# Adaptive vectors by row sums on the Vector engine, from transposed weights

## The chip, the core and the metric

One core of a Trainium2 chip runs the whole program: one launch of some 21,000 instructions, all unrolled, on PE (matrix products), DVE (vector), ACT (scalar functions and copies) and POOL, with SP issuing most of the transfers. The metric is device time in microseconds. The kernel before takes 1334.85 us, the median of 3 runs (1333.11 to 1336.33).

## The reference

Two layers work on 512 latent tokens of width 1024, with 256 context tokens as a prefix. Layer 0 mixes by neighbourhood attention and a two-way gated recurrence (HGRN2), layer 1 by a short gated convolution; each ends in a convolutional gated feed-forward part. What matters here is the conditioning of each layer:

```
silu_c = jax.nn.silu(c)                              # (1, 1024)
mod = silu_c @ ada_w[layer] + ada_b[layer]           # ada_w[layer]: 1024 x 6144
shift_m, scale_m, gate_m, shift_f, scale_f, gate_f = jnp.split(mod, 6, axis=-1)
h = modulate(rms_norm(x, norm_mix_w[layer]), shift_m, scale_m)
x = x + gate_m[:, None, :] * y
h = modulate(rms_norm(x, norm_ffn_w[layer]), shift_f, scale_f)
x = x + gate_f[:, None, :] * conv_ffn(h, ...)
```

So each layer has six adaptive vectors of 1024 values, which are one product of a row with a 1024 x 6144 matrix.

## The kernel before

Activations lie transposed: 8 tiles of 128 channels by 512 tokens. A value per channel is then a value per partition, and `mod[:, l, c]` holds the 128 values of column block `c` (0 to 47) of layer `l`: shift_m is c 0 to 7, scale_m 8 to 15, gate_m 16 to 23, shift_f 24 to 31, scale_f 32 to 39, gate_f 40 to 47.

Each product of full precision runs as three PE matmuls (`mm3`, lines 287 to 290), on weights and activations that are split into a high and a low part. `Weights` loads the raw weights on SP's queue into two buffers (`wraw`); ACT casts the high part (line 92 or 125) and DVE subtracts it to get the low part (line 93 or 126), into three buffers of each. `get` and `ahead` set how far the splitting runs ahead of PE. A raw buffer can be loaded again when its last split on DVE is done.

In order of time: a prefix (norm, shift_m and scale_m of layer 0 on PE by `ada_tile`, the first projections `pq`), the projections and scans of the recurrence, the attention, the output projection, ffn_up of layer 0, ffn_down of layer 0 (`project_back` with `kgroups`, 640 to 760 us), od_in (the three projections of the short convolution, 760 to 950 us), od_out, ffn_up of layer 1, ffn_down of layer 1. Every engine works its instructions in order, and that order is set by a list scheduler that goes by program order and readiness; `pin` keeps an instruction behind all that were written before it on its engine.

The other adaptive vectors (the last four of layer 0, all six of layer 1) are worked out piece by piece beside all this, by the class `Ada` (lines 474 to 527). A job is 512 outputs, 20 jobs in all. One unit (`unit`) takes 128 of the 1024 inputs: SP loads 128 x 512 weights (`ar`, three buffers, loaded two units ahead), and DVE multiplies them by the 128 values of silu(c), one per partition (`sil[:, r, 0:1]`), and adds them to `aa` (line 504; line 502 for the first of a job). After 8 units DVE reduces `aa` across 32 partitions with a transposing reduction (line 508, `ad`), three calls later PE sums the four groups of partitions by a small product with `sel` (line 514, `gather`, `pad`), and two calls later DVE adds the bias in four pieces (line 520, `finish`). The reduction, the gather and the sums are not pinned.

Units are called from fixed places. `Weave` calls a unit after so many ticks of the projections (`ada_units`, lines 563 and 948); from the output projection on, `units(n)` stands between other work: in `project_back` (line 1053) behind the two weight tiles of a step and ahead of its products, in od_in behind each pair of tiles (lines 1283, 1291, 1300), and in ffn_up of layer 1 (line 1252).

At the end of ffn_up of layer 1 (lines 1319 to 1325) gate_f is laid out along the rows of all partitions: DVE multiplies the identity by 128 values, PE multiplies a matrix of ones by that diagonal, ACT copies the result out of PSUM.

Of the kernel before, what the change touches and what calls it, by code (L numbers as in the profile page):

```python
# [9 lines left out]
F32 = mybir.dt.float32  # L10
F32R = mybir.dt.float32r
BF16 = mybir.dt.bfloat16
I32 = mybir.dt.int32
# [161 lines left out]
def backbone(ctx: ExitStack, tc: tile.TileContext, a, out, dump=None):  # L175
# [65 lines left out]
    ws = Weights(nc, wp, plan)  # L241


    cst = cp.tile([P, 769], F32, name="cst")
    ident, sel = cst[:, 0:128], cst[:, 128:256]
    smask = cst[:, 256:769]
    hgm = cp.tile([P, 256], I32, name="hgm")
    ones = cp.tile([P, P], F32, name="ones")
    epsc = cp.tile([P, 1], F32, name="epsc")
    V.memset(ones[:], 1.0)  # L250
# [2 lines left out]
    vec = cp.tile([P, 372], F32, name="vec")  # L253
    pv, abT, fcv = vec[:, 0:100], vec[:, 100:196], (vec[:, 196:284], vec[:, 284:372])
    mod = cp.tile([P, 3, 48], F32, name="mod")
    sil = cp.tile([P, 8, 32], F32, name="sil")
    oml = cp.tile([P, 8], F32, name="oml")
    noml = cp.tile([P, 8], F32, name="noml")
    amul = cp.tile([P, 5, KT], F32, name="amul")
# [2 lines left out]

    m1 = ExitStack()
    mp = m1.enter_context(tc.tile_pool(name="mp", bufs=1))
    y0 = [yp.tile([P, 2, T], F32R, tag=f"y{k}", name=f"h0_{k}") for k in range(KT)]
    h0 = [(t[:, 0], t[:, 1]) for t in y0]
    hc4 = [mp.tile([P, 4, TC], F32R, tag="hc", name=f"hc{i}", bufs=4) for i in range(4)]
# [61 lines left out]
    with ExitStack() as st:  # L329
# [94 lines left out]
        for k in range(KT):  # L424
            fetch(k + 2)
            if k == 3:
                for i in range(2):
                    nc.sync.dma_start(ct[i][:].rearrange("p (k t) -> p k t", t=TC),
                                      ctxt[i * T : (i + 1) * T, :].rearrange("(k p) t -> p k t", p=P))
                nc.sync.dma_start(hgm[:], a["hgm"])  # L430
                nc.sync.dma_start(cst[:, 256:769], a["cst"][:, 256:769])
            conv(k + 1)
            modulated(h0[k][0], h0[k][1], xs[k][:], 0, k)
            if k + 1 < KT:
                ada_tile(k + 1, k + 2)
            wh, wl = w0[k]
            for m in range(6):
                ms = slice(m * P, (m + 1) * P)
                mm3(pq[m][:], wh[:, ms], wl[:, ms], h0[k][0], h0[k][1], k == 0, k == KT - 1)
                if k > 6 or (k == 6 and m % 2):  # L440
                    next(ctx_task, None)
                if k == KT - 1 and m in (2, 4):
                    ws.conv()
# [14 lines left out]
        for m in range(4):  # L458
            sg = sp.tile([P, T], F32, tag="sgq", name=f"sgq{m}", bufs=2)
            S.activation(sg[:], pq[m][:], AF.Sigmoid)  # L460
            V.tensor_tensor(qf[m], pq[m][:], sg[:], ALU.mult)
        for m in range(2):
            gate(m, pq[4 + m][:])
        for _ in ctx_task:
# [9 lines left out]
    class Ada:  # L474


        jobs = [(0, p_, j) for p_ in range(2, 6) for j in range(2)] + [(1, p_, j) for p_ in range(6) for j in range(2)]
        n, calls, raw, late = 0, 0, {}, []

        def load(self):  # L480
            n = len(self.raw)
            r = n % 8
            l, p_, j = self.jobs[n // 8]
            raw = ap_.tile([P, T], F32, tag="araw", name=f"ar{n}", bufs=3)
            nc.sync.dma_start(raw[:], ada_w[l][r * P : (r + 1) * P, p_ * D + j * T : p_ * D + (j + 1) * T])
            self.raw[n] = raw

        def unit(self, aux):
            self.calls += 1
            while self.late and self.late[0][0] <= self.calls:  # L490
                self.late.pop(0)[1]()
            if self.n >= 8 * len(self.jobs):
                return
            r = self.n % 8
            l, p_, j = self.jobs[self.n // 8]
            while len(self.raw) < min(self.n + 3, 8 * len(self.jobs)):
                self.load()
            raw = self.raw[self.n]
            self.n += 1
            if r == 0:  # L500
                self.acc = ap_.tile([P, T], F32, tag="aacc", name=f"aa{self.n}", bufs=1)
                pin(V.tensor_scalar(self.acc[:], raw[:], sil[:, 0, 0:1], None, ALU.mult))
                return
            pin(V.scalar_tensor_tensor(self.acc[:], raw[:], sil[:, r, 0:1], self.acc[:], ALU.mult, ALU.add))  # L504
            if r < 7:
                return
            red = ap_.tile([P, 16], F32, tag="ared", name=f"ad{self.n}", bufs=1)
            V.tensor_reduce(red[:], self.acc[:].rearrange("p (b j) -> p b j", j=32), axis=AX.X, op=ALU.add,
                            apply_transpose=True)
            pm = []  # L510

            def gather():
                pm.append(aux(f"pad{l}{p_}{j}"))
                TE.matmul(pm[0][:, 0:16], sel, red[:], start=True, stop=True)

            def finish():
                c = p_ * 8 + 4 * j
                for qd in range(4):
                    s4 = slice(32 * qd, 32 * qd + 32)
                    V.tensor_tensor(mod[s4, l, c : c + 4], pm[0][s4, qd:16:4], abT[s4, l * 48 + c : l * 48 + c + 4],  # L520
                                    ALU.add)
                if p_ in (1, 4):
                    w0 = (16 if p_ == 1 else 32) + 8 * l + 4 * j
                    V.scalar_tensor_tensor(amul[:, 2 * l + (1 if p_ == 1 else 2), 4 * j : 4 * j + 4], mod[:, l, c : c + 4],
                                           1.0, pv[:, w0 : w0 + 4], ALU.add, ALU.mult)

            self.late += [(self.calls + 3, gather), (self.calls + 5, finish)]

    ada = Ada()

# [25 lines left out]

    def ada_units(n, gap):
        for _ in range(n):
            ada.unit(aux_t)
            yield gap  # L560


    wv.add(ada_units(11, 6))
    for j in range(2):
        pl = [acc_t(f"pvl{j}{i}") for i in range(2)]
        pcx = aux_t(f"pvc{j}")
# [378 lines left out]

    wv.add(attention())
    wv.add(gated(), 20)
    wv.add(ada_units(43, 3))
    for p_ in range(1, 4):
        query(p_)  # L950
        key_value(p_)
# [83 lines left out]
    def project_back(nm, src, groups, gate, norm, start=0):  # L1035
# [5 lines left out]
        for n, (mp_, gi) in enumerate(steps):  # L1041
            k0, k1 = groups[gi]
            if gi == 0:
                o = [acc_t(f"pb{nm}{mp_}{i}") for i in range(2)]
            w = [ws.get(), ws.get()]
            first, lastg = gi == 0, gi == len(groups) - 1
            if n == len(steps) - 1:
                break
            if n == len(steps) - 2:
                ws.spare = [(gq, f"q{2 * i}", f"q{2 * i + 1}") for i in range(3)]  # L1050
                ws.ahead(4)
            if n < len(steps) - 2 or len(groups) > 1:
                units(4 if len(groups) == 1 else 5)
            for i in range(2):
                mms(o[i], w[i], src, k0, k0, k1, slice(0, T), first, lastg)
                if lastg:
                    norm.back(o[i], 2 * mp_ + i, slice(0, T), gate)
                    if mp_ or i:
                        norm.add(slice(0, T))
# [162 lines left out]

    def units(n):
        for _ in range(n):
            ada.unit(aux_t)

    def ffn_up(l, src, rest):
        g = []
        mv = []

        def gated_tile(f, oa, ov):
            col = lambda n: fcv[l][:, n : n + 1]
            tt = fp.tile([P, T], F32, tag="t", name=f"cv{l}{f}", bufs=5)
            conv3(tt, oa, col(f), col(22 + f), col(44 + f), col(66 + f))
            S.activation(tt[:], tt[:], AF.Gelu)
            gh, gl = gtiles(l, f)
            V.tensor_tensor(ov[:], ov[:], tt[:], ALU.mult)
            split(gh, gl, ov[:])
            g.append((gh, gl))

        def before():
            rest()
            mv.extend(differences(l, src))

        oa, ov = quad(f"a{l}", src, before, lambda: mv[1]())
        for i in range(2):
            gated_tile(i, oa[i], ov[i])
        for j in range(1, FT // 2):
            for i, (ra, rv) in enumerate(group(f"{l}{j}", mv[0])):
                gated_tile(2 * j + i, ra, rv)  # L1250
            if l and j < 9:
                units(2)
        return g

    mix = [mixn[p_] for p_ in range(4)] + [mixg[h] for h in range(4)]
# [22 lines left out]
    for j in range(4):  # L1278
        if j == 0:
            oc, ou = quad("c", nrm.h, rest)  # L1280
        else:
            oc = pair(f"c{j}", nrm.h)
            units(3)
        cs = []
        for i in range(2):
            t = gp.tile([P, T], F32, tag=f"g{16 + i}", name=f"cs{j}{i}")
# [1 line left out]
            cs.append(t)  # L1288
        if j:
            ou = pair(f"u{j}", nrm.h)  # L1290
            units(3)
        ts_ = []
        for i in range(2):
            m = 2 * j + i
# [2 lines left out]
            conv3(t, cs[i], rowv(76 + m, 1), rowv(84 + m, 1), rowv(92 + m, 1), rowv(68 + m, 1))  # L1297
            ts_.append(t)
        ob = pair(f"b{j}", nrm.h)
        units(3)  # L1300
        for i in range(2):
            m = 2 * j + i
            mh = gp.tile([P, T], F32R, tag=f"g{2 * m}", name=f"mch{m}")
# [79 lines left out]
def layout(inputs):  # L1383
# [5 lines left out]
    for l in range(2):  # L1389
# [3 lines left out]
    arrays["upq"] = np.ascontiguousarray(np.stack([  # L1393
        np.concatenate([blk(0, 2, 1), blk(2, 4, 1), blk(0, 2, 0), blk(2, 4, 0)], -1),
        np.concatenate([blk(4, 8, 0), blk(4, 8, 1)], -1)], 2))
    arrays["vec"] = np.ascontiguousarray(np.concatenate([np.asarray(v).reshape(-1, P) for v in vecs], 0).T)
    rpb = np.asarray(inputs["na_rpb"])[0].reshape(4, 2, 15, 31)
    rp = np.zeros((4, 15, 2, WPAD), rpb.dtype)
# [29 lines left out]
```

## Time and profile before

| what | value |
|---|---|
| runs, median of 3 | 1334.85 us (1333.11 to 1336.33) |
| the profiled execution | 1333.99 us, of which the span from first to last instruction is 1332.2 us |
| PE busy | 98% of the span |
| weight loads of PE | 86% |
| DVE busy | 72% |
| ACT busy | 47% |
| mean DMA rate | 129 GB/s |
| mean granted clock of PE | 0.995 of full speed |

A busy share is an average over stages with different limits, and a PE that is busy by the records is not always at its peak, since matmuls overlap each other: the distance between the starts of two matmuls says what one costs. Idle time of an engine counts only where another waits for it at the end of a chain. The page cuts the span into 40 slices; stages are read with windows.

### The profile page before, as it was taken

The numbers are of one execution on the slowest core, as the hardware profiler recorded it, in microseconds if no ns is written. First come the engines' busy times: TensorE is split into PE (matmuls) and PEld (weight loads), VectorE is DVE, ScalarE is ACT, GpSimd is POOL, SyncE is SP. The second block draws the span as 40 slices with busy tenths as digits, with TensorE's granted clock in tenths as the row PEclk, the third lists the DMA queues.
The fourth block names the chain that finished last, engine by engine and source line by source line (L and its number), as shares of the span: only waits on it lengthen the run. The fifth ranks groups of instructions, "written<-read, shape, count | busy, mean of one in ns | idle before, by whom it ended". The sixth has DMA issues, their size and how long they took to land. (4 is left out here: it accounts for less than half of the span.)

```text
span 1332.2 us, 21229 instructions
## 1 busy us (share of the span) xinstructions
PE 1304.5 (98%) x8456; PEld 1147.6 (86%) x8456; DVE 965.4 (72%) x1688; ACT 625.2 (47%) x1085; POOL 84.3 (6%) x87
## 2 busy tenths in 40 slices
PE   7999999999999999999999999999999999999997
PEld 4798888888779998889877898888999989899997
DVE  4668897887778878788766776667789897782333
ACT  4443445555545656565422253223456565663223
POOL 2204332311000000000000000000000000000000
PEclk9999999999999999999999999999999999999999
DMA  9842113674562122323466734555403423242231
GB/s 293 265 123 84 33 33 82 152 182 134 153 206 96 64 99 92 127 71 119 141 211 198 226 132 143 167 165 174 158 27 117 142 80 127 80 146 69 91 108 64
DMA packets 134995, 172.35 MB, mean 129 GB/s; under 512 B 14320, under 2 KB 103792, under 8 KB 129776
## 3 DMA queue, kind: packets, MB, share of 16 engines
q1 hardware_dynamic: 132896, 166.15, 39.3%
q10 hardware_dynamic: 2000, 4.85, 1.4%
q8 instruction: 66, 1.08, 0.3%
q14 instruction: 33, 0.27, 0.1%
HBM read 165.21 MB, written 2.10 MB: 126 GB/s over the span
## 5 line engine op out<-in xcount | busy, mean ns | idle before, releaser
L92 ACT CAST whi<-wraw 128x1024 fp32r<-128x1024 f32 (+1 forms) x122 | 124.1, 1021 | 280.8 <-PE pd L1340 70.4
L93 DVE TENSOR_TENSOR wlo<-wraw,whi 128x1024 fp32r<-128x1024 f32 (+1 forms) x122 | 145.2, 1192 | 107.7 <-ACT whi L92 107.1
L288 PE MATMUL p<-hf,whi 128*128 128x512 f32 (+1 forms) x640 | 215.4, 338 | 1.4 <-ACT whi L125 1.4
L290 PE MATMUL p<-hf,wlo 128*128 128x512 f32 (+1 forms) x640 | 214.6, 335 | 0.0
L289 PE MATMUL p<-hf,whi 128*128 128x512 f32 (+1 forms) x640 | 214.1, 335 | 0.0
L125 ACT CAST whi<-wraw 128x512 fp32r<-128x512 f32 (+1 forms) x160 | 113.0, 727 | 85.0 <-PE p L289 35.0
L290 PEld LDWEIGHTS p<-hf,wlo 128*128 128x128 f32 x640 | 120.1, 188 | 13.6
L288 PEld LDWEIGHTS p<-hf,whi 128*128 128x128 f32 x640 | 120.1, 188 | 12.3 <-ACT whi L125 1.6
L289 PEld LDWEIGHTS p<-hf,whi 128*128 128x128 f32 x640 | 120.1, 188 | 10.7
L126 DVE TENSOR_TENSOR wlo<-wraw,whi 128x512 fp32r<-128x512 f32 (+1 forms) x160 | 128.1, 817 | 0.9 <-ACT whi L125 0.5
L504 DVE SCALAR_TENSOR_TENSOR aa<-ar,sil,aa 128x512 f32<-128x512 f32 x140 | 104.8, 749 | 24.1 <-DMA ar<-in_ada_w_dram 21.8
L1339 PE MATMUL pd<-whi,g 128*128 128x256 f32 x352 | 98.2, 279 | 0.0
L1341 PE MATMUL pd<-wlo,g 128*128 128x256 f32 x352 | 98.1, 279 | 0.0
L1340 PE MATMUL pd<-whi,g 128*128 128x256 f32 x352 | 97.9, 278 | 0.0
L288 PE MATMUL pbd<-g,whi 128*128 128x512 f32 (+1 forms) x192 | 73.5, 383 | 0.0
L289 PE MATMUL pbd<-g,whi 128*128 128x512 f32 (+1 forms) x192 | 73.3, 382 | 0.0
L290 PE MATMUL pbd<-g,wlo 128*128 128x512 f32 (+1 forms) x192 | 73.1, 381 | 0.0
L288 PE MATMUL p<-T,whi 128*128 128x256 f32 x240 | 69.0, 288 | 0.0
L290 PE MATMUL p<-T,wlo 128*128 128x256 f32 x240 | 67.2, 280 | 0.0
L289 PE MATMUL p<-T,whi 128*128 128x256 f32 x240 | 67.2, 280 | 0.0
L1340 PEld LDWEIGHTS pd<-whi,g 128*128 128x128 f32 x352 | 66.3, 188 | 0.0
L1339 PEld LDWEIGHTS pd<-whi,g 128*128 128x128 f32 x352 | 66.1, 188 | 0.0
(679 smaller groups left out, 3296.3 us busy)
## 6 DMA issues: line engine op xcount, KB each, us to landing
ar<-in_ada_w_dram SPq DMA_DIRECT2D x160, 256.0 KB, 3.1
wraw<-in_upq_dram SPq DMA_DIRECT2D x40, 1024.0 KB, 4.8
wraw<-in_ffn_w_down_dram SPq DMA_DIRECT2D x16, 1024.0 KB, 5.3
wraw<-in_od_w_in_dram SPq DMA_DIRECT2D x12, 1024.0 KB, 5.6
wraw<-in_ev_w_in_dram SPq DMA_DIRECT2D x20, 512.0 KB, 5.2
araw<-in_ada_w_dram SPq DMA_DIRECT2D x16, 512.0 KB, 6.3
wraw<-in_ffn_w_down_dram SPq DMA_DIRECT2D x8, 768.0 KB, 4.7
wraw<-in_ev_w_out_dram SPq DMA_DIRECT2D x4, 1024.0 KB, 6.9
```

Source lines behind the costliest of these rows:

```text
L92: self.nc.scalar.copy(hv, rv)
L93: self.pin(self.nc.vector.tensor_tensor(lv, rv, hv.bitcast(F32), ALU.subtract))
L125: self.nc.scalar.copy(hi, src)
L126: V.tensor_tensor(lo, src, hi.bitcast(F32), ALU.subtract)
L288: TE.matmul(o, wh, mh, start=start, stop=False, skip_group_check=True)
L289: TE.matmul(o, wh, ml, start=False, stop=False, skip_group_check=True)
L290: TE.matmul(o, wl, mh, start=False, stop=stop, skip_group_check=True)
L504: pin(V.scalar_tensor_tensor(self.acc[:], raw[:], sil[:, r, 0:1], self.acc[:], ALU.mult, ALU.add))
L1339: TE.matmul(o[i][:, 0:256], gh[:, ts], w[0][:, k - k0], start=k == 0, stop=False)
L1340: TE.matmul(o[i][:, 0:256], gl[:, ts], w[0][:, k - k0], start=False, stop=False)
L1341: TE.matmul(o[i][:, 0:256], gh[:, ts], w[1][:, k - k0], start=False, stop=k == FT - 1)
```

## The change

The weights of the adaptive vectors are passed a second time, transposed: `adaT[l, c]` is 128 outputs by 1024 inputs, one contiguous block. A job is now one column block `c`, 80 in all, and one unit: SP loads 128 x 1024 weights (two buffers, one unit ahead), and one DVE operation multiplies them by silu(c), which lies in the row of every partition (`silr`, 1024 values), sums each row, starts from the bias and writes the 128 results to `mod[:, l, c]`. Reduction, gather, sums and the late calls are gone. `silr` is made once in the prefix, behind the first projections, by the pattern of lines 1319 to 1325: eight diagonals on DVE, eight products with ones on PE in two PSUM tiles, two copies on ACT. The number of units per call is halved, about, at each place. Some constants (`sil`, `hgm`, the scan mask) move to the pool `mp`, which ends after the attention part.

```diff
-    cst = cp.tile([P, 769], F32, name="cst")
+    cst = cp.tile([P, 256], F32, name="cst")
...
+    sil = mp.tile([P, 8, 32], F32, name="sil")
+    hgm = mp.tile([P, 256], I32, name="hgm")
+    smt = mp.tile([P, 513], F32, name="smt")
+    smask = smt[:]
+    silr = ap_.tile([P, D], F32, name="silr")
...
@@ behind the sigmoids of pq
+        for j in range(2):
+            pt = aux_t(f"psr{j}")
+            for r in range(4):
+                dg = sp.tile([P, P], F32, tag="dgs", name=f"dgs{j}{r}", bufs=2)
+                V.tensor_scalar(dg[:], ident, sil[:, 4 * j + r, 0:1], None, ALU.mult)
+                TE.matmul(pt[:, r * P : (r + 1) * P], ones[:], dg[:], start=True, stop=True, skip_group_check=True)
+            S.copy(silr[:, j * T : (j + 1) * T], pt[:])
...
@@ class Ada
-        jobs = [(0, p_, j) for p_ in range(2, 6) for j in range(2)] + [(1, p_, j) for p_ in range(6) for j in range(2)]
+        jobs = [(0, c) for c in range(16, 48)] + [(1, c) for c in range(48)]
...
+            l, c = self.jobs[len(self.raw)]
+            raw = ap_.tile([P, D], F32, tag="araw", name=f"ar{len(self.raw)}", bufs=2)
+            nc.sync.dma_start(raw[:], a["adaT"][l, c])
...
+            while len(self.raw) < min(self.n + 2, len(self.jobs)):
                 self.load()
             raw = self.raw[self.n]
+            l, c = self.jobs[self.n]
             self.n += 1
...
-            pin(V.scalar_tensor_tensor(self.acc[:], raw[:], sil[:, r, 0:1], self.acc[:], ALU.mult, ALU.add))
...
-            V.tensor_reduce(red[:], self.acc[:].rearrange("p (b j) -> p b j", j=32), axis=AX.X, op=ALU.add,
-                            apply_transpose=True)
...
-                TE.matmul(pm[0][:, 0:16], sel, red[:], start=True, stop=True)
...
-                    V.tensor_tensor(mod[s4, l, c : c + 4], pm[0][s4, qd:16:4], abT[s4, l * 48 + c : l * 48 + c + 4],
-                                    ALU.add)
...
+            pin(V.tensor_tensor_reduce(raw[:], raw[:], silr[:], 1.0, abT[:, l * 48 + c : l * 48 + c + 1], ALU.mult,
+                                       ALU.add, mod[:, l, c : c + 1]))
+            if c in (15, 39):
+                w0 = (16 if c == 15 else 32) + 8 * l
+                V.scalar_tensor_tensor(amul[:, 2 * l + (1 if c == 15 else 2), :], mod[:, l, c - 7 : c + 1], 1.0,
+                                       pv[:, w0 : w0 + 8], ALU.add, ALU.mult)
...
-    wv.add(ada_units(11, 6))
+    wv.add(ada_units(6, 11))
...
-    wv.add(ada_units(43, 3))
+    wv.add(ada_units(21, 6))
...
@@ project_back
-                units(4 if len(groups) == 1 else 5)
+                units(2)
...
@@ ffn_up of layer 1
-                units(2)
+                units(1)
...
@@ od_in, at three places
-            units(3)
+            units(2)
...
+    arrays["adaT"] = np.ascontiguousarray(np.asarray(inputs["ada_w"]).reshape(2, D, 48, P).transpose(0, 2, 3, 1))
```

## Rows read from the trace of the kernel before

**Rows 1.** Engine totals on the page: busy us, share of the span, instructions.

```profile
...
PE 1304.5 (98%) x8456; PEld 1147.6 (86%) x8456; DVE 965.4 (72%) x1688; ACT 625.2 (47%) x1085; POOL 84.3 (6%) x87
...
```

**Rows 2.** Windows by stage: busy us per engine, granted clock, DMA share, GB/s.

```profile
...
230.00:420.00 190.00, 186.91 (x1259) 158.48 (x1259) 147.44 (x311) 105.51 (x198) 22.81 (x24) 1.00 0.56 162
...
640.00:760.00 120.00, 116.28 (x517) 94.94 (x516) 82.35 (x127) 32.40 (x40) 0.00 (x0) 0.97 0.64 201
760.00:950.00 190.00, 190.00 (x977) 161.85 (x977) 130.04 (x200) 66.22 (x90) 0.00 (x0) 1.00 0.53 167
...
```

**Rows 3.** Waits of PE, whole span: us in total, times, longest.

```profile
...
PE pad L514 <- DVE ad L508: 3.7, 2, 1.9
PE pkc L626 <- DVE sc L609: 2.2, 2, 1.5
...
```

**Rows 4.** Timeline of PE, 105 to 108 us: start us, us, instruction.

```profile
...
106.44 0.39 PE L289 MATMUL pf<-h,whi 128*128 128x512 f32 x1
...
106.90 0.29 PE L514 MATMUL pad<-ad,cst 128*128 128x16 f32 x2
...
107.59 0.40 PE L290 MATMUL pf<-h,wlo 128*128 128x512 f32 x1
...
```

**Rows 5.** Timeline of all engines, 655 to 690 us.

```profile
...
666.11 1.54 DVE L504 SCALAR_TENSOR_TENSOR aa<-ar,sil,aa 128x512 f32<-128x512 f32 x2 [2.94 <-DMA ar<-in_ada_w_dram]
666.16 0.39 PE L290 MATMUL pbd<-g,wlo 128*128 128x512 f32 x1
...
668.45 0.40 PE L514 MATMUL pad<-ad,cst 128*128 128x16 f32 x2 [1.91 <-DVE ad L508]
...
668.70 0.48 PE L288 MATMUL pbd<-g,whi 128*128 128x512 f32 x1
...
672.66 0.39 PE L289 MATMUL pbd<-g,whi 128*128 128x512 f32 x1
...
```

**Rows 6.** Timeline of PE, 700 to 707 us.

```profile
...
699.86 0.40 PE L289 MATMUL pbd<-g,whi 128*128 128x512 f32 x1
...
706.71 0.39 PE L290 MATMUL pbd<-g,wlo 128*128 128x512 f32 x1
...
```

**Rows 7.** Timeline of PE, 1196 to 1204 us.

```profile
...
1196.89 0.60 PE L1324 MATMUL pgb<-dgb,ones 128*128 128x128 f32 x4
...
1197.57 0.28 PE L1341 MATMUL pd<-wlo,g 128*128 128x256 f32 x1
...
1198.05 0.29 PE L1339 MATMUL pd<-whi,g 128*128 128x256 f32 x1
...
```

**Rows 8.** DVE by line and form: count, busy us, mean ns, idle before.

```profile
...
L93 DVE TENSOR_TENSOR wlo<-wraw,whi 128x1024 fp32r<-128x1024 f32 x110 | 134.8, 1228 | 83.3 <-ACT whi L92 82.7
L504 DVE SCALAR_TENSOR_TENSOR aa<-ar,sil,aa 128x512 f32<-128x512 f32 x140 | 104.8, 749 | 24.1 <-DMA ar<-in_ada_w_dram 21.8
...
L874 DVE CUSTOM_DVE_ANT_0 ps<-ps,bm,sm 128x256 f32<-128x256 f32 x32 | 15.3, 488 | 0.7
...
L508 DVE TRANSPOSE_TENSOR_REDUCE ad<-aa 128x16 f32<-128x512 f32 x20 | 14.2, 710 | 0.5
...
L520 DVE TENSOR_TENSOR mod<-pad,vec 32x4 f32<-32x4 f32 x80 | 12.5, 156 | 4.1 <-PE pad L514 2.9
...
L502 DVE TENSOR_SCALAR aa<-ar,sil 128x512 f32<-128x512 f32 x20 | 10.2, 508 | 3.6 <-DMA ar<-in_ada_w_dram 3.2
...
L874 DVE DVE_READ_ACCUMULATOR2_ANT sm<- 128x1 f32 x32 | 4.3, 134 | 0.1
...
L1323 DVE TENSOR_SCALAR dgb<-cst,mod 128x128 f32<-128x128 f32 x8 | 2.0, 282 | 0.4 <-PE pgb L1324 0.4
...
```

**Rows 9.** DMA issues: count, KB each, median us to landing.

```profile
...
wraw<-in_ev_w_in_dram SPq DMA_DIRECT2D x20, 512.0 KB, 5.2
...
```

**Rows 10.** Timeline of all engines, 60 to 100 us.

```profile
...
65.33 0.28 PE L577 MATMUL pvl<-whi,h 128*128 128x256 f32 x1
...
```

**Rows 11.** Instructions of tile gb: count, ns minimum/median/maximum.

```profile
...
L1325 ACT COPY gb<-pgb x2: 587/587/587, 1201.3 to 1203.2; 128x512 f32<-128x512 f32 x2
...
```

More of the change, by code (lines that the diff above doesn't have):

```diff
@@ L241, in backbone @@
     ws = Weights(nc, wp, plan)
-    cst = cp.tile([P, 769], F32, name="cst")
+    cst = cp.tile([P, 256], F32, name="cst")
     ident, sel = cst[:, 0:128], cst[:, 128:256]
-    smask = cst[:, 256:769]
-    hgm = cp.tile([P, 256], I32, name="hgm")
     ones = cp.tile([P, P], F32, name="ones")
@@ L255, in backbone @@
     mod = cp.tile([P, 3, 48], F32, name="mod")
-    sil = cp.tile([P, 8, 32], F32, name="sil")
     oml = cp.tile([P, 8], F32, name="oml")
@@ L430, in backbone @@
                 nc.sync.dma_start(hgm[:], a["hgm"])
-                nc.sync.dma_start(cst[:, 256:769], a["cst"][:, 256:769])
+                nc.sync.dma_start(smt[:], a["cst"][:, 256:769])
             conv(k + 1)
@@ L474, in backbone @@
     class Ada:
-        jobs = [(0, p_, j) for p_ in range(2, 6) for j in range(2)] + [(1, p_, j) for p_ in range(6) for j in range(2)]
-        n, calls, raw, late = 0, 0, {}, []
+        jobs = [(0, c) for c in range(16, 48)] + [(1, c) for c in range(48)]
+        n, raw = 0, []
         def load(self):
[L481 to L492, printed above, removed]
+            l, c = self.jobs[len(self.raw)]
+            raw = ap_.tile([P, D], F32, tag="araw", name=f"ar{len(self.raw)}", bufs=2)
+            nc.sync.dma_start(raw[:], a["adaT"][l, c])
+            self.raw.append(raw)
+        def unit(self):
+            if self.n >= len(self.jobs):
                 return
-            r = self.n % 8
-            l, p_, j = self.jobs[self.n // 8]
-            while len(self.raw) < min(self.n + 3, 8 * len(self.jobs)):
+            while len(self.raw) < min(self.n + 2, len(self.jobs)):
@@ L497, in unit @@
                 self.load()
             raw = self.raw[self.n]
+            l, c = self.jobs[self.n]
             self.n += 1
[L500 to L503, printed above, removed]
-            pin(V.scalar_tensor_tensor(self.acc[:], raw[:], sil[:, r, 0:1], self.acc[:], ALU.mult, ALU.add))
-            if r < 7:
-                return
@@ L507, in unit @@
-            red = ap_.tile([P, 16], F32, tag="ared", name=f"ad{self.n}", bufs=1)
-            V.tensor_reduce(red[:], self.acc[:].rearrange("p (b j) -> p b j", j=32), axis=AX.X, op=ALU.add,
-                            apply_transpose=True)
-            pm = []
-            def gather():
-                pm.append(aux(f"pad{l}{p_}{j}"))
-                TE.matmul(pm[0][:, 0:16], sel, red[:], start=True, stop=True)
[L516 to L519, printed above, removed]
-                    V.tensor_tensor(mod[s4, l, c : c + 4], pm[0][s4, qd:16:4], abT[s4, l * 48 + c : l * 48 + c + 4],
-                                    ALU.add)
[L522 to L525, printed above, removed]
@@ L527, in unit @@
-            self.late += [(self.calls + 3, gather), (self.calls + 5, finish)]
+            pin(V.tensor_tensor_reduce(raw[:], raw[:], silr[:], 1.0, abT[:, l * 48 + c : l * 48 + c + 1], ALU.mult,
[4 more added lines that the diff above has]
+                                       pv[:, w0 : w0 + 8], ALU.add, ALU.mult)
@@ L558, in ada_units @@
         for _ in range(n):
-            ada.unit(aux_t)
+            ada.unit()
             yield gap
-    wv.add(ada_units(11, 6))
+    wv.add(ada_units(6, 11))
     for j in range(2):
@@ L1224, in units @@
         for _ in range(n):
-            ada.unit(aux_t)
+            ada.unit()
     def ffn_up(l, src, rest):
@@ L1290, in backbone @@
             ou = pair(f"u{j}", nrm.h)
-            units(3)
+            units(2)
         ts_ = []
@@ L1299, in backbone @@
         ob = pair(f"b{j}", nrm.h)
-        units(3)
+        units(2)
         for i in range(2):
```

## The prediction

> **What bounds the kernel now.** I read the engine totals first, then the windows by stage, then the list of PE's waits, and only then the timelines at those waits. The totals [rows 1] put PE at 1304.5 us of a span of 1332.2 us, DVE at 965.4 us. So time is won or lost only where PE has an instruction more or less, stands still, or runs at the lower clock; a saving on DVE counts only where PE waits for DVE. The windows [rows 2] show two stages that matter here. In the attention stage (230 to 420 us) PE is busy for 186.9 of 190 us and DVE for 147.4, with the clock at 1.00. In the first ffn_down stage (640 to 760 us) PE loses 3.7 us and the granted clock is 0.97 where the others have 1.00, and the DMA moves 201 GB/s; in the od_in stage behind it (760 to 950 us) PE loses nothing. The waits of PE [rows 3] name the place: `pad` (line 514, the gather matmul of the adaptive vectors) waits twice for `ad` (the DVE reduction of line 508), 3.7 us in all. The next wait on DVE, `pkc`, is 2.2 us and belongs to another part.
>
> **The change part by part.**
>
> *The gather matmuls go from PE.* There are 20 (160 units, one gather for each 8), each issued as two instructions of 16 columns. In the timeline of an undisturbed one [rows 4], two matmuls of 512 columns take 106.44 to 106.90, 0.23 us each; from the gather at 106.90 to the matmul at 107.59 lie the gather and two such matmuls, 0.69 us, so the gather costs 0.69 - 0.46 = 0.23 us. For the 18 without a wait that is 18 x 0.23 = 4.1 us, with nothing beside them that hides it: PE's stream is full.
>
> *The two gathers that wait.* In the first [rows 5] DVE stands 2.94 us for the transfer of `ar`, so the reduction is late; PE's matmul at 666.16 is followed by the gather at 668.45, after 1.91 us idle, and the next large matmul at 668.70. [...] From 666.16 to 672.66 are eleven steps, 6.50 us where 2.53 were due: 3.97 us lost, the gather included. The second [rows 6] is the same: 699.86 to 706.71, thirteen steps, 6.85 us where 2.99 were due, 3.86 us lost. Together 7.8 us. Both go, because after the change a unit ends in a column of `mod` on DVE and no PE instruction reads its result directly; what is late instead is DVE alone (below).
>
> Removed from PE: 4.1 + 7.8 = 11.9 us.
>
> *PE's new work.* Eight 128-column fp32 matmuls (ones times a diagonal) fill `silr`, 16 instructions, the same pattern as lines 1322 to 1325. There [rows 7] four such instructions and two 256-column matmuls take 1196.89 to 1197.57, 0.68 us; four 256-column matmuls take 0.48 us, so the four instructions cost 0.68 - 0.24 = 0.44 us, and sixteen 1.8 us. Between two large matmuls a pair would cost what the gather's pair does, 8 x 0.23 = 1.8 us too. The lower bound is nothing: the diagonals need only `ident` and `sil`, ready early, and if the matmuls are drawn forward into an idle moment of PE before 13 us they are free. I take 1.8 us.
>
> *DVE.* Before: 104.8 + 10.2 + 14.2 + 12.5 = 141.7 us for products, first products, reductions and sums with the bias [rows 8]. After: 80 units. No row shows this operation at 1024 elements out of SBUF. The nearest are the plain product of 1024 (line 93, 1.228 us) and the same custom operation at 256 elements, one operand in PSUM (line 874, 0.488 us), with its accumulator read of 0.134 us [rows 8]. Below, a unit costs 1.23 us; above, four times the row of 256 and the read, 4 x 0.488 + 0.134 = 2.09 us. I take 1.228 + 0.134 = 1.36 us, as line 874's length is near that of plain operations of 256. 80 x 1.36 = 109 us, so DVE gains 33 us and PE nothing from it, as it waits for DVE little [rows 3].
>
> [...] Line 504 reads two fp32 operands from SBUF and takes 0.749 us for 512, and line 874 keeps one operand in PSUM [rows 8], so the trace has no accumulating operation with both in SBUF. [...]
>
> *Transfers and the SP queue.* The same 40 MB come as 80 transfers of 512 KB in place of 160 of 256 KB, in whole rows of 4 KB. Two buffers of 1024 replace three of 512. In the first ffn_down stage a step had 5 units (1.25 MB) and now has 2 (1 MB), so that stage carries less beside its weights; od_in has 2 units a group where 3 were, 1 MB for 0.75 MB, in a stage without loss [rows 2]. The second unit of a pair now waits on a transfer that SP issues after the previous pair's second unit and behind one weight transfer, which itself waits for a DVE split half a step earlier. A step of 8 k tiles lasts 48 x 0.23 = 11.0 us, a 512 KB transfer 5.2 us [rows 9], more behind 1 MB of weights, so DVE may stand some microseconds at the second unit. Queued behind it on DVE are the next weight split and the residual sum; the split's tile is due on PE a step later, 11 us, which covers it. If that cover failed, PE would stall as in rows 5 and 6.
>
> *Due times.* Attention ends with 27 units done where 54 half units were; the gate of ffn_down (columns 40 to 47) needs 32 units, and 33 are done two steps into that stage, before the first residual sum. Each later consumer likewise has its column before it asks. I cost this at nothing.
>
> *Prefix.* ACT gets two copies of 512 columns, DVE eight diagonals; the first projection's matmul has no idle time before it [rows 10], so PE has no room there. Its cost if not hidden is the first rival.
>
> *Sum,* against the profiled execution: 1333.99 - 11.9 + 1.8 = 1323.9 us. The median of the runs lies 0.9 us above that execution (1334.85), so 1324.7 us.
>
> **Rivals.**
>
> *The prefix waits.* The diagonals have two buffers, and the first projection's accumulator may lie in the bank that `psr` used. If PE alternates with DVE, each diagonal costs 0.28 us [rows 8] and 0.23 us in turn, 8 x 0.51 = 4.1 us; a copy of 0.59 us [rows 11] frees the bank; a drop of the clock as in rows 5 adds 1.7. That is 6.4 us for the 1.8 counted: 1324.7 + 4.6 = 1329.3 us. For it: the diagonals come behind sigmoid products on an in-order DVE. Against: at line 1324 the same pattern ran without PE waiting.
>
> *The stalls return elsewhere.* The wait for the second unit of a pair pushes a weight split past its cover, twice: 7.8 us come back, 1332.5 us, no change. For it: DVE already waits for these transfers. Against: the 11 us of cover.
>
> *Slower: the unit runs at half rate and holds up the softmax.* If the operation takes two cycles where line 93's takes one, a unit lasts 2 x 1.228 + 0.134 = 2.59 us. In the attention stage 21 units take 54.4 us where 43 old ones took 43/160 of 141.7 = 38.1, 16.3 us more; in the first projections six take 15.5 for 9.7, 5.8 more. These stages have PE instructions that wait for DVE (the scans' `sc`, the softmax row). If two thirds of the 22.1 us land on PE: 1324.7 + 14.7 = 1339.4 us. It decides from 12.9 us on. Against: DVE has 42.6 us idle in the attention window [rows 2], and PE hardly waits for it. [...]
>
> **How the numbers follow.** A run of this kernel tells 0.2% (2.7 us) from no change, so faster ends at 1332.2 and slower begins at 1337.5. Forecast as summed: 0.50. Prefix waits: 0.20. Stalls return: 0.13. Half rate with PE waiting: 0.12. A small rest of 0.05, a changed order of instructions in the scan stage, I split over the three. Faster 0.50 + 0.20 + 0.03 = 0.73; same 0.14; slower 0.13. The forecast's own range is 1321 to 1328 (1.8 us free, or a few waits of PE for DVE gone with DVE's lighter load; the prefix partly exposed). The range that should hold 8 times in 10 reaches from 1320, through the prefix and the returned stalls, to 1336.
>
> **What would show it.** Right: no instruction on PE that waits for a unit; the clock of 640 to 760 us at 1.00 and PE idle there near nothing; that window's work done about 9 us sooner; 16 new PE instructions before 70 us with little idle beside them; a unit near 1.36 us on DVE. Wrong: a unit near 2.6 us with `pt` or `pkc` waiting longer; PE idle at 65 us behind `psr`; a low clock at some new place; weight splits in the ffn_down stage that PE waits for.

## The result and the profile after

The kernel after takes 1338.05 us (median of 20 runs, 1335.65 to 1340.15); the kernel before took 1335.97 us beside it (20 runs, 1333.11 to 1339.95). The ratio is 1.0017, 95% interval 1.0010 to 1.0024: a loss of 2.1 us, where a gain of 10.1 us was forecast. The time lies outside the forecast's range. The profiled execution of after took 1338.84 us, with a span of 1336.9 us, 4.7 us longer than the span of before.

The engine totals of after, to be held against [rows 1]:

```profile
PE 1307.8 (98%) x8432; PEld 1153.3 (86%) x8432; DVE 930.8 (70%) x1593; ACT 624.9 (47%) x1087; POOL 85.0 (6%) x87
```

PE has 24 instructions less, as counted (40 gone, 16 new), and yet is busy for 3.3 us more. DVE has lost 34.6 us (33 were forecast).

The windows of after by stage, columns as in [rows 2], with the prefix (60 to 130 us) added:

```profile
60.00:130.00 70.00, 64.92 (x445) 60.31 (x444) 42.72 (x75) 27.98 (x49) 5.29 (x7) 0.95 0.39 120
230.00:420.00 190.00, 186.94 (x1265) 155.78 (x1266) 134.03 (x273) 104.09 (x190) 28.11 (x27) 1.00 0.56 163
640.00:760.00 120.00, 120.00 (x566) 100.15 (x566) 74.89 (x105) 39.54 (x56) 0.00 (x0) 1.00 0.56 182
760.00:950.00 190.00, 190.00 (x979) 163.03 (x978) 126.45 (x186) 68.15 (x92) 0.00 (x0) 1.00 0.55 178
```

The first ffn_down stage is as forecast: PE no longer idle, clock 1.00 instead of 0.97. From its first product (`pbd`) to the first of od_in (`ppc`) it took 131.1 us before and 121.5 now. The rows of the two families, before and then after, give first and last start (us) behind the durations:

```profile
L288 PE MATMUL pbd<-g,whi x192: 276/392/628, 652.5 to 783.3; 128*128 128x512 f32 x160, 128*128 128x256 f32 x32
L288 PE MATMUL ppc<-hm,whi x112: 276/280/476, 783.6 to 894.2; 128*128 128x256 f32 x64, 128*128 128x512 f32 x48
```

```profile
L290 PE MATMUL pbd<-g,whi x192: 276/389/467, 665.9 to 787.1; 128*128 128x512 f32 x160, 128*128 128x256 f32 x32
L290 PE MATMUL ppc<-hm,whi x112: 276/283/467, 787.4 to 896.7; 128*128 128x256 f32 x64, 128*128 128x512 f32 x48
```

But the stage begins 13.4 us late. The window of 60 to 130 us shows where most of that is from: PE loses 5.1 of 70 us and the granted clock is 0.95. Before, the same window had a clock of 1.00:

```profile
60.00:130.00 70.00, 67.83 (x493) 62.78 (x492) 53.63 (x88) 30.36 (x55) 12.55 (x13) 1.00 0.42 124
```

PE's waits of after, columns as in [rows 3]:

```profile
PE psr L470 <- DVE dgs L469: 4.2, 2, 4.1
PE pkc L608 <- DVE sc L591: 2.3, 2, 1.5
```

`pad` is gone; `psr`, the products that make `silr`, wait for their diagonals in its place. PE's timeline there (start us, us, instruction, idle time before it):

```profile
66.15 0.61 PE L470 MATMUL psr<-dgs,ones 128*128 128x128 f32 x4
66.91 0.49 PE L470 MATMUL psr<-dgs,ones 128*128 128x128 f32 x2 [0.16 <-DVE dgs L469]
71.47 3.25 PE L470 MATMUL psr<-dgs,ones 128*128 128x128 f32 x10 [4.07 <-DVE dgs L469]
74.37 0.56 PE L559 MATMUL pvl<-whi,h 128*128 128x256 f32 x1
74.73 0.41 PE L560 MATMUL pvl<-whi,h 128*128 128x256 f32 x1
...
77.50 0.31 PE L561 MATMUL pvl<-wlo,h 128*128 128x256 f32 x1
77.65 0.27 PE L559 MATMUL pvl<-whi,h 128*128 128x256 f32 x1
77.76 0.28 PE L560 MATMUL pvl<-whi,h 128*128 128x256 f32 x1
```

From the first `psr` to the first product of the next projection are 8.22 us, 4.2 of them waits. The last ten instructions take 2.90 us of it, at a granted clock of 0.58 (70 to 74.3 us); without waits ten take 1.2 (first experiment). How much of that is the clock and how much the diagonals that were still to come, isn't separated. The fifteen steps from 74.37 to 77.65 take 3.28 us where 0.12 us each, the pitch behind them, would be 1.8: the granted clock there is 0.52 (1.00 from 77.65 to 85 us), and these steps, behind the idle time, take 1.5 us more. DVE's timeline in that stretch:

```profile
66.57 0.29 DVE L469 TENSOR_SCALAR dgs<-cst,sil 128x128 f32<-128x128 f32 x1 [0.74 <-PE psr L470]
66.77 0.68 DVE L463 TENSOR_TENSOR qh<-pq,sgq 128x512 f32<-128x512 f32 x1
...
69.94 1.28 DVE L463 TENSOR_TENSOR qh<-pq,sgq 128x512 f32<-128x512 f32 x2
71.14 0.47 DVE L469 TENSOR_SCALAR dgs<-cst,sil 128x128 f32<-128x128 f32 x2
71.53 0.74 DVE L282 SCALAR_TENSOR_TENSOR gg<-pq,vec,gg 128x512 f32<-128x512 f32 x1
72.30 0.29 DVE L469 TENSOR_SCALAR dgs<-cst,sil 128x128 f32<-128x128 f32 x1
```

The first two diagonals were made as soon as `sil` was there, at 11.22 and 11.53 us. The third needs a buffer that PE has read, so it can start only at 66.57; the fourth's buffer comes free soon after, but it starts at 71.14, behind 4.4 us of other work on DVE (sigmoid products, the context's norm).

DVE by line and form, columns as in [rows 8]:

```profile
L93 DVE TENSOR_TENSOR wlo<-wraw,whi 128x1024 fp32r<-128x1024 f32 x110 | 134.8, 1229 | 120.6 <-ACT whi L92 120.1
L504 DVE CUSTOM_DVE_ANT_0 ar<-ar,silr,vec 128x1024 f32<-128x1024 f32 x80 | 100.6, 1279 | 3.7 <-DMA ar<-in_adaT_dram 3.7
...
L504 DVE DVE_READ_ACCUMULATOR2_ANT mod<- 128x1 f32 x80 | 6.5, 82 | 0.0
```

A unit takes 1.279 + 0.082 = 1.36 us, the value taken, though by luck in the parts: the operation is 51 ns longer than its term (1.228), the read of the accumulator 52 ns shorter (0.134). And DVE waits 3.7 us in all for its transfers, against 25.0 before (21.8 at line 504, 3.2 at line 502 [rows 8]); they land in 3.9 us:

```profile
ar<-in_adaT_dram SPq DMA_DIRECT2D x80, 512.0 KB, 3.9
```

The end of the kernel shows a second loss. The products `pd` of the last stage, before and then after: duration ns minimum/median/maximum, first and last start us.

```profile
L1340 PE MATMUL pd<-whi,g x352: 276/276/366, 1197.5 to 1324.7; 128*128 128x256 f32 x176
```

```profile
L1322 PE MATMUL pd<-whi,g x352: 276/283/365, 1199.2 to 1329.4; 128*128 128x256 f32 x176
```

The line and its operands are the same, yet the median is 283 ns instead of 276, and the stage takes 130.2 us instead of 127.2 by these rows. The 192 products `pvl` in the prefix show the same (276 before, 283 now). Nothing in the forecast has such a term.

### The profile page after: what moved, and what is told of

It reads as the page before. It is cut to its first block, busy times and chain, and to the rows that moved or that the text cites. A ratio compares the mean times of both kernels' runs of the same rounds, so it can differ in the third digit from the quotient of the medians.

```text
span 1336.9 us, 20838 instructions
## 1 busy us (share of the span) xinstructions
PE 1307.8 (98%) x8432; PEld 1153.3 (86%) x8432; DVE 930.8 (70%) x1593; ACT 624.9 (47%) x1087; POOL 85.0 (6%) x87
## 4 chain that ended last, share of the span: by engine, by line
PE 82%; DVE 9%; ACT 3%; DMA 3%; issue 1%; SPq 0%; ACTq 0%; DVEq 0%
PE p L290 10%; PE p L291 9%; PE p L292 9%; PE pbd L291 3%; PE pbd L292 3%; PE pbd L290 3%; PE pd L1321 3%; PE pd L1323 3%; PE pd L1322 3%; PE pbo L290 1%; PE pbo L292 1%; PE pbo L291 1%; PE ppc L292 1%; PE ppc L290 1%; PE ppc L291 1%
## 5 line engine op out<-in xcount | busy, mean ns | idle before, releaser
L504 DVE CUSTOM_DVE_ANT_0 ar<-ar,silr,vec 128x1024 f32<-128x1024 f32 x80 | 100.6, 1279 | 3.7 <-DMA ar<-in_adaT_dram 3.7
L290 PE MATMUL pbd<-g,whi 128*128 128x512 f32 (+1 forms) x192 | 71.7, 373 | 0.0
L291 PE MATMUL pbd<-g,whi 128*128 128x512 f32 (+1 forms) x192 | 71.5, 372 | 0.0
L290 PE MATMUL p<-T,whi 128*128 128x256 f32 x240 | 68.8, 287 | 0.0
L1323 PEld LDWEIGHTS pd<-wlo,g 128*128 128x128 f32 x352 | 67.2, 191 | 0.0
```

The lines of the kernel that those rows point to most:

```text
L290: TE.matmul(o, wh, mh, start=start, stop=False, skip_group_check=True)
L291: TE.matmul(o, wh, ml, start=False, stop=False, skip_group_check=True)
L504: pin(V.tensor_tensor_reduce(raw[:], raw[:], silr[:], 1.0, abT[:, l * 48 + c : l * 48 + c + 1], ALU.mult, ALU.add, mod[:, l, c : c + 1]))
L1323: TE.matmul(o[i][:, 0:256], gh[:, ts], w[1][:, k - k0], start=False, stop=k == FT - 1)
```

## The experiments

Three questions: does the wait for the diagonals account for the prefix, were the waiting gathers the loss of the first ffn_down stage, and what makes `pd` longer? All ratios are to the kernel before, run beside each kernel on the same chip.

**Eight buffers for the diagonals.**

```diff
-                dg = sp.tile([P, P], F32, tag="dgs", name=f"dgs{j}{r}", bufs=2)
+                dg = sp.tile([P, P], F32, tag="dgs", name=f"dgs{j}{r}", bufs=8)
```

> The changed kernel with eight buffers in place of two for the diagonals of silr, nothing else. Theory A (PE waits for diagonals that have no free buffer until PE has used the two before, and that stand on DVE behind the sigmoid products): all eight are made before 15 us, the 16 instructions of psr take about 2 us in place of 8.2 and the clock stays at 1.00 behind them; 9 us go, 1329 us. Rival B (the 12 us late at 104 us come from the units' own transfers and the tighter DVE, and psr only fills a pause that would be there anyway): psr shortens but the first projection ends no earlier, within 2 us of 1338.

Measured: 1331.27 us, ratio 0.9967 (0.9956 to 0.9978), 6.8 us less than after (9 were expected). PE's timeline:

```profile
65.88 1.95 PE L470 MATMUL psr<-dgs,ones 128*128 128x128 f32 x16
68.49 0.38 PE L559 MATMUL pvl<-whi,h 128*128 128x256 f32 x1 [0.66 <-ACT silr L471]
68.71 0.28 PE L560 MATMUL pvl<-whi,h 128*128 128x256 f32 x1
```

All sixteen run without a gap in 1.95 us, and the products `pvl` behind them go at 0.12 us each from 68.71 on. What is left is 0.66 us for ACT's copy, the bank of the rival's second term.

**No product at all.** The row of c is broadcast to all partitions by a transfer, and ACT's sigmoid and a DVE product make `silr`; the loop over the diagonals is left out.

```diff
+        nc.sync.dma_start(crow[:], bass.AP(csrc.tensor, csrc.offset, [[0, P], [1, D]]))
...
+        pin(S.activation(silr[:], crow[:], AF.Sigmoid))
+        pin(V.tensor_tensor(silr[:], crow[:], silr[:], ALU.mult))
```

> The changed kernel with silr made without PE: the row c is sent to all partitions by one transfer of 512 KB, ACT takes its sigmoid and DVE the product, both behind the gates of the first projections. Theory A: the first projection follows the last pq matmul with no gap, so 8.2 us of psr and some 2 us of low clock behind it go: 1327 to 1328 us, about 2 us below the run with eight diagonals. Rival B: no change against the changed kernel, 1338. Rival C (the extra transfer and 1.2 us each of ACT and DVE at that place delay the weight splits): 1332 to 1336.

Measured: 1329.47 us, ratio 0.9958 (0.9945 to 0.9971), where 1327 to 1328 were expected. The first `pvl` is at 66.6 us. With the first experiment this shows that the products for `silr` cost some 8 us (8.6 by the medians, 7.9 by the ratios), and that most of it is the wait for buffers.

**The kernel before with `psr`, result unused.**

```diff
+    silr = mp.tile([P, D], F32, name="silr")
...
+                dg = sp.tile([P, P], F32, tag="dgs", name=f"dgs{j}{r}", bufs=2)
```

> The kernel before with the block that makes silr added at the place of the change and with two buffers, its result used by nobody; the units are the old ones. Theory A: the block alone costs what the changed kernel lost by 104 us, 9 to 12 us: 1345 to 1348. Rival B (the loss comes with the new units): within 2 us of 1336.

Measured: 1344.09 us, ratio 1.0064 (1.0043 to 1.0084), some 8.5 us more (9 to 12 were expected). Its waits of PE hold the new loss and the old one side by side:

```profile
PE psr L469 <- DVE dgs L468: 4.2, 2, 4.1
PE pad L523 <- DVE ad L517: 4.1, 2, 2.3
```

So the new loss needs nothing of the change but these lines. The median of its `pd` is 277 ns: the second loss isn't in it.

**The kernel before with a later gather.** The stalls in the first ffn_down stage removed without the change.

```diff
-            self.late += [(self.calls + 3, gather), (self.calls + 5, finish)]
+            self.late += [(self.calls + 6, gather), (self.calls + 7, finish)]
```

> The kernel before with each gather six calls behind its reduction in place of three (and the sums seven), nothing else. Theory D (two gathers stall PE in the first ffn_down stage because the reduction is late, and the clock falls behind each): both waits go, the clock of 640 to 760 us is 1.00, 7.3 us less: 1328.7. Rival E (the stall belongs to the stage, as its transfers are late, and only moves to another instruction): within 2 us of 1336, PE still idle in that window.

Measured: 1338.93 us, ratio 1.0028 (1.0016 to 1.0040): slower, not what either theory expected. Its windows and PE's longest wait:

```profile
230.00:420.00 190.00, 181.51 (x1199) 152.30 (x1197) 142.78 (x301) 100.12 (x185) 23.33 (x24) 0.99 0.54 156
640.00:760.00 120.00, 119.58 (x565) 99.35 (x564) 87.64 (x137) 37.80 (x53) 0.00 (x0) 1.00 0.61 195
```

```profile
PE pbo L288 <- DVE xT L1002: 6.1, 1, 6.1
```

The stage gives back 6.6 us (131.1 to 124.5), so the gathers' waits were its loss. But PE now stands still in front of a product of the output projection that starts at 420.36. Rows of PE, ACT and DVE there:

```profile
420.36 0.58 PE L288 MATMUL pbo<-mnh,whi 128*128 128x256 f32 x1 [6.11 <-DVE xT L1002]
407.77 2.00 ACT L92 CAST whi<-wraw 128x1024 fp32r<-128x1024 f32 x2 [3.15 <-DMA wraw<-in_ffn_w_up_dram]
408.86 2.36 DVE L93 TENSOR_TENSOR wlo<-wraw,whi 128x1024 fp32r<-128x1024 f32 x2 [3.17 <-ACT whi L92]
416.10 0.69 DVE L108 TENSOR_TENSOR ws<-wraw 128x512 f32<-128x512 f32 x1 [1.35 <-DMA wraw<-in_upq_dram]
419.83 0.48 DVE L1002 SCALAR_TENSOR_TENSOR xT<-pbo,mod,xT 128x256 f32<-128x256 f32 x1
```

The residual sum (line 1002) that PE waits for stands on DVE behind splits of weights, and these wait for transfers of raw weights, not for a unit. SP issued those transfers later than in the kernel before, behind five of the units' (`ar`) in one piece. SP's rows, before and then with the later gather:

```profile
386.50 3.75 SPq L485 DMA_DIRECT2D ar<-in_ada_w_dram  x3
392.05 0.38 SPq L63 DMA_DIRECT2D wraw<-in_ffn_w_up_dram  x1
```

```profile
390.52 10.61 SPq L485 DMA_DIRECT2D ar<-in_ada_w_dram  x5
402.72 2.77 SPq L63 DMA_DIRECT2D wraw<-in_ffn_w_up_dram  x2
```

It is like the rival "the stalls return elsewhere", in another kernel: DVE in order, and a transfer at its head. That the later transfers alone make the 6.1 us is read from these rows; no run tested it.

**Thirty-two bytes in front of the weights.** The kernels differ in where their buffers start, since constants have left the first pool. By the kernels' memory plans (the addresses that the build gives to the tiles) the weight buffers begin at 9152 bytes in each partition before and at 5024 after. My first theory was that this start counts (a multiple of 64 before, 32 above one after); 32 unused bytes shift it, in three kernels:

```diff
+    padc = cp.tile([P, 8], F32, name="padc")
+    V.memset(padc[:], 0.0)
```

> The changed kernel with nothing but 32 unused bytes per partition behind the constants, set to zero once, so that the weight buffers of the column GEMMs start at 5056 instead of 5024 bytes in each partition (a multiple of 64, as 9152 in the kernel before; 5024 is 32 above one). Theory L (where the weight buffers start sets the rate of the products pvl and pd): pd falls from a mean of 282-283 ns to 278-280 and the last stage from 130.5 to 127.5 us, pvl from 283 to 276 ns and 28.6 to 27 us, and the kernel from 1338.1 to 1333.5 us, near ratio 0.998 against the kernel before. Theory R (the rate comes from elsewhere, as from the transfers beside them or from the weights' order, and the start does nothing): 1338 us, last stage 130.5 us. Both: psr still takes 8 us.

> The kernel before with the same 32 unused bytes, which put its weight buffers at 9184 bytes, 32 above a multiple of 64; nothing else differs. Theory L: it pays what the changed kernel pays: pd 282-283 ns, last stage 130.5 instead of 127.5 us, pvl 283 ns, and 1340 us in all, ratio 1.003. Theory R: 1335.5 us, ratio 1.000, pd 278-280 ns.

> The kernel with the row of c broadcast by a transfer and no product for it (1329.5 us), with the 32 bytes. Theory L: pvl and pd give back 4.5 us: 1325 us, ratio 0.992 against the kernel before, last stage 127.5 us. Theory R: 1329.5 us, ratio 0.996.

Measured: 1341.44 us, ratio 1.0047 (1.0030 to 1.0064); 1335.13 us, 1.0002 (0.9989 to 1.0016); 1332.94 us, 0.9983 (0.9973 to 0.9994). The theory fell three times: the kernel before didn't mind, and the two others got slower by 3.4 and 3.5 us, where the theory had 4.5 us less. But that the start does nothing wasn't right either. So I took the pitch (the distance between two starts) of every product from the traces, and set it beside the distance of the start addresses of its two operands in the memory plans: the one of 128 columns that the product's weight load has (PEld, mean 188 ns for `pd` before), here called the held one, and the one of 256 or 512 columns that its matmul has, the moved one. The means in ns, worked out from the traces, by that distance modulo 256 bytes (the count of products of one kernel behind them is 766 to 768 where not given):

| product, columns | 0 | 64 | 96 | 128 | 192 |
|---|---|---|---|---|---|
| `pd`, 256 | 120.0 after, 119.9 after + 32 bytes | 114.1 after (276) | 119.4 before (275), 119.7 after + 32 bytes (277) | 118.3 before + 32 bytes (275) | 113.6 before, 113.6 before + 32 bytes |
| `pvl`, 256 (178 to 192) | 120.0 after | | | | 113.5 before |
| `ppb`, 512 (192) | 226.8 after | 229.8 before | | | |

In one trace the pitch changes with the tile that is multiplied: in after, `pd` has 114.1 for the six tiles that lie in a pool of their own and 120.0 for the other sixteen; before it was 119.4 and 113.6. In `pd` the weights are moved, the activations are held; neither's own start decides. The 32 bytes move the weights and the sixteen tiles together, and their pitch stays (120.0 and 119.9, 113.6 and 113.6); the pool of the six stays where it is, so their distance goes from 64 to 96 in the changed kernel and their pitch from 114.1 to 119.7, which is 1.6 of the 3.4 us.

**Sixty-four bytes between the weights and the pools above.** This moves the activations against the weights, and so the distance.

```diff
     wp = ctx.enter_context(tc.tile_pool(name="wp", bufs=2))
+    bp = ctx.enter_context(tc.tile_pool(name="bp", bufs=1))
...
+    padw = bp.tile([P, 16], F32, name="padw")
+    V.memset(padw[:], 0.0)
```

> The kernel with c's row broadcast and no product for it, with 64 unused bytes per partition between the weight buffers and the pools above them (not the 32 bytes of the constants). Theory M, formed from the pitches of the nine traces so far: with 256 moving columns the pitch of a product follows the distance of its two operands' start addresses modulo 128 bytes, 113.3 to 114 ns at 64, 120 at 0, 118 to 120 at 32 and 96; with 512 columns 227 at 0 and 229 to 230 at 64. The 64 bytes put the distance of nearly all products with 256 columns at 64: pd at 113.4 ns throughout, 1056 of them 120 us instead of 124.7; pvl at 113.4 instead of 120; the sum over all products 4.4 us less than without the bytes, so 1325 us, ratio 0.992. Theory R (any shift of the buffers costs, as the 32 bytes did): 1331 us or more.

> The changed kernel with nothing but the 64 bytes between the weight buffers and the pools above. Theory M: pd and pvl as above (pitch 113.4 ns), the last stage 126 instead of 130.6 us; 4.4 us less than 1338.1, so 1333.7 us, ratio 0.998; psr takes its 8 us as ever. Theory R: 1338 to 1341.5 us.

> The kernel before with the 64 bytes, which turn its distances of 64 into 0: theory M has pd at 120 ns for k from 6 on (767 of its products), pvl at 120, products with 512 columns 2 to 3 ns shorter; summed over all products 8 us more with values taken over for three small families, and at least 5: 1340.5 to 1343.5 us, ratio 1.004 to 1.006. Theory R: also slower, but by the same 3 us or so and with another pattern of pitches; no effect: 1335.5 us.

Measured: 1326.31 us, ratio 0.9933 (0.9914 to 0.9952); 1334.96 us, 0.9999 (0.9987 to 1.0011), 3.1 us under after (2.4 by the ratios); 1347.93 us, 1.0095 (1.0076 to 1.0115). `pd` in the changed kernel and in the kernel before, with the bytes:

```profile
L1325 PE MATMUL pd<-whi,g x352: 276/276/365, 1201.7 to 1326.6; 128*128 128x256 f32 x176
```

```profile
L1343 PE MATMUL pd<-whi,g x352: 274/281/368, 1209.3 to 1340.4; 128*128 128x256 f32 x176
```

In the changed kernel the stage falls from 130.2 to 124.9 us, its products at a mean pitch of 113.4 ns. In the kernel before the same bytes lengthen it from 127.2 to 131.1. That the placement of the activations against the weights sets the pitch of `pd` is shown in both directions. The size for the kernel before was missed: 11 us where 5 to 8 were expected, as I had formed the distance modulo 128. Its distance is 128 modulo 256, and there the products with 512 columns go at 233.5 ns (`ppb`), not at the 227 that they have at 0.

**Both repairs, and the best version again.** Eight diagonals and the 64 bytes; beside it the version without products for `silr` and with the 64 bytes.

> Both repairs of the changed kernel together: eight buffers for the diagonals and the 64 bytes between the weight buffers and the pools above. If the two losses are apart from each other, the 6.8 us that the eight buffers gave (1331.3 for 1338.1) and the 3 to 4.4 us that the 64 bytes gave add up: 1327 to 1328 us, ratio 0.993 to 0.994 against the kernel before, psr consecutive and pd at a pitch of 113.4 ns. If they overlap (the low clock behind psr slowing the same products pvl), 1329 us.

> The kernel with c's row broadcast and the 64 bytes once more, beside the one with eight diagonals and the 64 bytes on the same chip: 1326 to 1327 us, 1 to 2 us ahead of that one, which still issues psr's 16 instructions (1.8 us) on TensorE.

Measured: 1328.93 us, ratio 0.9944 (0.9925 to 0.9964), and 1327.51 us, 0.9933 (0.9913 to 0.9953). By the medians the second is 1.4 us ahead, as expected, but their intervals overlap. The first lies above the 1327 to 1328 us of adding up, at the 1329 of the other case; by the ratio it fits either, so the run does not decide between them. Both beat the kernel before and after; the version with the broadcast row is the best found by the median, 0.67% below the kernel before.

## Why the prediction was wrong

**The step that failed first: "I take 1.8 us"** for PE's new work. The sixteen instructions themselves were sized well: 1.95 us without waits. But they took 8.2 us, and the products behind them 1.5 us more at the low clock (0.52), 9.7 in all, 7.9 over the term. This is the rival "the prefix waits" (chance 0.20, 6.4 us), and its price was too low as well. The 1.7 us that it adds for a drop of the clock are 1.66 in the trace of before (ten steps from 668.70 to 672.66 in 3.96 us, where 0.23 each would be 2.30, at a granted clock of 0.57); behind `psr` it was 1.5. The rival let each diagonal cost its own 0.28 us and a product in turn; what it left out is that with two buffers the diagonals from the third on can't be made early, although their inputs are ready at 11 us, so they come to DVE in the middle of other work and queue behind it. The forecast's argument against it, the pattern of lines 1319 to 1325 that ran without a wait [rows 7], had the same two buffers, but a quieter DVE beside it: there DVE stood idle for 0.4 us until PE had read a diagonal [rows 8], so no other work stood in front.

**The term that wasn't in the sum:** the move of constants was given no cost. It changed the distances between weights and activations. `pd` lost 3.0 us and `pvl` some 1.2 (192 x 6.5 ns); products with 512 columns gained some 2 ns each, 1.1 us in od_in and 0.9 in the first ffn_down stage. Summed over all products by their mean pitches it is some 3.2 us of loss.

**What held.** The waiting gathers: the stage is 9.6 us shorter; with 0.8 us of that from the pitches, and 0.9 from the four other gathers in it (0.23 each by the forecast), 7.9 are left for the 7.8 forecast. DVE's unit: 1.36 us as taken. Transfers and due times: no PE wait for a unit, 3.7 us of DVE waiting. The rival of half rate, a supposition of the author's that no row showed, did not happen: this unit has both its fp32 operands in SBUF, writes an accumulator and takes 1279 ns for 1024, 51 ns longer than the plain operation of 1024 in line 93 [rows 8], where twice line 93 would be 2456 ns.

**The sum, mended:** 1324.7 + 7.9 (`psr`) + 3.2 (distances) = 1335.8 us; the kernel before ran 1.1 us above its first median in the later comparison, which makes 1336.9 against 1338.05 measured. The two traces lie further apart than the medians: 4.7 us, where the mended sum has 1.0. Of the rest 0.8 us is the prefix up to `psr` [rows 10], which I didn't pursue; over the fourteen traces the last product of `ada_tile` (`pm`), which stands ahead of `psr`, starts between 57.6 and 59.6 us (58.1 before, 59.0 after), so this much lies within what single executions differ by. The larger part, 2.6 us, stays open: between 240 and 666 us the kernel after goes from 12.2 to 13.4 us behind, although the six gathers there are gone, for which the forecast had 1.4 us. With eight diagonals it loses there too (4.9 to 6.7), in the kernel before with `psr` it doesn't (11.5 to 11.1). So it belongs to the new units or to the distances, which no run here separates for this stretch.

Taking both losses away gives 7.3 us less than the kernel before; the forecast had 10.1.

## What to carry to other kernels

The helper with two buffers, produced on DVE and consumed on PE, cost the queue of the producer (8.2 us), not the length of its instructions (1.95 us): ask what stands there when a buffer comes free, or give it as many buffers as it has pieces. A change that resizes a pool moves every buffer behind it (here the weights from 9152 to 5024 bytes): compare the pitch of unchanged products line by line before looking for a cause in what was changed. If it moved, look at the distance of the operands' addresses (`pd` for sixteen of its tiles: 113.6 ns at 192 before, 120.0 at 0 after).

## What the hardware showed that was not expected

In these traces the pitch of PE's products changed with the distance, modulo 256 bytes, between the start addresses of the moved and the held operand in SBUF. `pd` and `pvl`, with 256 columns, had 113.3 to 114 ns at 64 and 192, 120 at 0, 118 to 120 at 96 and 128; `ppb`, with 512 columns, 226.8 at 0, about 229.5 at 64, 233.5 at 128. It is not a full rule: `ppa` and `ppc` have 114.1 to 114.4 at 64 in the kernels before and after, but 117.6 at 64 with the 64 bytes and without `psr`, and the products `p` with 256 columns differ little (some 118.5 at 64, 120 at 0). What the engine does there, and what else enters, stays open; it was worth some 3 to 11 us of 1336 in these kernels.
